# First stage and output products of a two-layer encoder trunk: rows turned by TensorE, written-out engine orders in the chunk loop, and a later place for the dilated heads' products

## The chip, the cores and the metric

The kernel runs on one core of a Trainium2 chip. A core has five engines that run their own instruction lists side by side: PE (TensorE, matmuls), ACT (ScalarE, functions and copies), DVE (VectorE, elementwise and reductions), POOL (GpSimd, elementwise from SBUF alone) and SP, which here only issues DMAs. They wait for each other by semaphores. The metric is the device time of one execution in microseconds (us), smaller is better.

## The reference, cut to what matters

Two layers of a bidirectional encoder on 512 tokens of width 1024. The conditioning vector c gives six vectors per layer (shift, scale and gate, twice).

```
c_act = silu(c)
for l in range(2):
    sh1, sc1, gt1, sh2, sc2, gt2 = split(c_act @ w_mod[l] + b_mod[l])
    h = rms_norm(x, g_norm_mix[l]) * (1 + sc1) + sh1
    q_d, k_d, v_d, cq, ckv, k_rope = split(h @ w_in[l])
    o_dil = dilated_attention(q_d, k_d, v_d, positions, slopes)   # 8 heads, biased by distance
    o_mla = latent_attention(cq, ckv, k_rope, positions, ...)     # 8 heads, rotary part with sin/cos
    x = x + gt1 * (concat[o_dil, o_mla] @ w_out[l])
    h = rms_norm(x, g_norm_mlp[l]) * (1 + sc2) + sh2
    x = x + gt2 * (square(relu(h @ w_mlp_in[l])) @ w_mlp_out[l])
```

## The kernel before, in words

x is kept transposed in SBUF as eight tiles of 128 features by 512 tokens. Every large product is made in float32 precision from three matmuls: each operand is split into a rounded high part and the rest, and `mm3` (lines 240 to 245) adds high times high (L241), one low part (L244) and the other low part (L245). `load_split` loads a weight tile by DMA into `raw` (or `zz`), ACT rounds it into `wh` (L233) and POOL makes the low part `wl` (L234).

**First stage (lines 86 to 154).** c is loaded column by column (`cs`), silu is made with Exp on ACT, and two matmuls with ones spread it over all partitions (`cb`). ACT squares the eight x tiles (L124, L127), DVE adds them up (L128) and a matmul with ones (L753) makes the sum of squares of each token. The positions are loaded as a column (`posc`), POOL makes and reduces the rotary angles (L135 to L147), ACT takes Abs and two Sin. Sin needs another function table than Exp and Ln: the table is loaded at L150 and put back at L152.

**Chunk loop of layer 0 (lines 750 to 780).** `inv_rms` (L250 to L256) turns the sum of squares into y = 1/rms: DVE scales the sum, ACT takes Ln (L252) and Exp (L253), DVE refines it in three steps. Then for each of eight chunks k of 128 features: DVE forms x times y (L759, L768), two modulation products with `cb`, one for shift and one for scale (L170, 128x1024 each), ACT makes the two columns from them (L194, L195), the rounded h (L772) and h in full (L773), and the low part of h is made by DVE for even chunks (L763) and by POOL for odd ones (L775). PE multiplies each chunk with the columns of W_in of the first pair of dilated heads (banks `mm`) and of the latent part (banks `sc` and `tr`), 24 matmuls in all, eight from each line of `mm3`. W_in comes in four double chunks, split by ACT and POOL (L233, L234). In this loop the order on DVE is the one in which the code is written (`tc.manual_schedule`); on all other engines, and everywhere else, the framework's list scheduler decides the order when the kernel is built. `W["tail"]` (L541 on) follows: turning the latent rows, the tables of the rotary part (`rope_tables`, L504 to L516, ten small POOL instructions called `rot`) and the rotated key (L559 to L562). `distances()` (L309 to L330) makes the distances between tokens.

**Pairs of heads.** Eight pairs of heads follow in each layer (`st` 0 to 7): four dilated pairs, four latent ones. A head has four blocks of 128 queries: scores on PE, maximum on DVE (L353), exponentials on ACT (L354), turning by PE (L365), split by ACT and DVE (L370, L371), values by PE (L377), and the head's end on DVE (L381). Beside pair st the next pair is prepared (`flow`), in layer 0 the other modulation products are made (`next_mod`), and the output product of the dilated heads, `out_dil(j)` for eight blocks j of 128 features, is put between: twelve matmuls of 128x512 each, and the addition to x on DVE (L670). `out_load(0, jj)` loads and splits its weights, two j each. `weave` and the numbers of TUNE say where in the program these stand: the number is how many blocks of the pair's two heads come first. The scheduler may move an instruction ahead of its place.

Of the kernel before, what the change touches and what calls it, by code (L numbers as in the profile page):

```python
# [42 lines left out]
def trunk(ctx: ExitStack, tc: tile.TileContext, a):  # L43
# [42 lines left out]
    cs = col(8, "cs")  # L86
    SY.dma_start(cs, a["c"].rearrange("(k p) -> p k", p=128))
    ident = const.tile([128, 128], F32, name="ident")
# [1 line left out]
    cols = [col(N_COL, f"cols{l}") for l in range(L)]  # L90
# [1 line left out]
    posc = const.tile([128, 4], I32, name="posc")
    SY.dma_start(posc, a["pos"].rearrange("(t p) -> p t", p=128))
    inv = col(16, "inv")
# [57 lines left out]
    pre = A.preload_act_table_set("natural_log_exp_and_others")  # L152
# [96 lines left out]
    def inv_rms(p, v, y, t):  # L249

        V.tensor_scalar(v, p, 1.0 / D, EPS, op0=OP.mult, op1=OP.add)
        A.activation(t, v, AF.Ln)  # L252
        A.activation(p, t, AF.Exp, scale=-0.5)  # L253
        V.tensor_tensor(t, v, p, op=OP.mult)
# [54 lines left out]
    def distances():  # L309

        posr = s2([128, S], I32)
        SY.dma_start(posr, bass.AP(tensor=a["pos"].tensor, offset=a["pos"].offset, ap=[[0, 128], [1, S]]))
        part = []
        for src, n, tile_ in ((posr, S, lambda dt: t4("pt", [128, 2, S], dt)),
                              (posc, 4, lambda dt: const.tile([128, 2, 4], dt, name=nm("pc")))):
            it, ft = tile_(I32), tile_(F32)
            V.tensor_scalar(it[:, 0], src, 16, None, op0=OP.arith_shift_right)
            V.tensor_scalar(it[:, 1], src, 65535, None, op0=OP.bitwise_and)
            V.tensor_copy(ft, it)
            part.append(ft)  # L320
        row, clm = part
# [66 lines left out]
    for l in range(L):  # L388
# [345 lines left out]
        if l == 0:  # L734
# [15 lines left out]
            with tc.manual_schedule(engines={mybir.EngineType.DVE}):  # L750
                for k in range(-1, 8):
                    if k < 0:
                        T.matmul(p, ones, sq0, start=True, stop=True)  # L753
# [10 lines left out]
                    if k < 7:  # L764
                        mod_block(0, k + 1, "ot", out=mraw[:, k + 1:k + 2])
                        if k < 0:
                            inv_rms(p, v, y, t)
# [6 lines left out]
                        if k % 2 == 0:  # L774
                            G.tensor_tensor(lo, u_of(k + 1), f(hi), op=OP.subtract)  # L775
# [213 lines left out]
```

## Time and profile before

| what | us |
|---|---|
| median of 3 runs | 1345.55 (1345.54 to 1348.59) |
| the profiled execution | 1343.71 |
| its span, first to last instruction | 1341.6 |
| start of the chunk loop's first matmul | 25.73 |
| start of the chunk loop's last matmul | 70.14 |
| end of head pair 1 / 4 / 8 in layer 0 (L381) | 134.2 / 227.9 / 331.2 |
| end of head pair 1 / 4 / 8 in layer 1 | 792.5 / 870.8 / 966.2 |

The profiled execution's time is 2.1 us longer than its span (what lies before the first and behind the last instruction) and 1.8 us under the median. The granted TensorE clock over the whole span is 0.984. A row of the timeline gives start, duration, engine, line, instruction and, in brackets, how long the engine had been idle and what ended that. A row of the windows gives for a stretch the busy time of PE, weight loads, DVE, ACT and POOL, the granted clock, the DMA share and rate.

### The profile page before, as it was taken

The page shows a single profiled execution, that of the slowest core. Times are in us where ns is not written, and L with a number is a line of the kernel's source. Part 1 is how long each engine was busy: PE and PEld are TensorE (multiplying, and loading weights), DVE is VectorE, ACT ScalarE, POOL GpSimd, SP SyncE. Part 2 cuts the span into 40 slices and gives each one's busy share as a digit, 9 for nine tenths or more (in the row PEclk, how much of TensorE's full clock was granted, in tenths as well). Part 3 has the DMA queues.
Part 4 walks back from the last instruction along what each step waited for, and adds up shares of the span by engine and source line. Part 5 has one row for each costly group of instructions (what it writes and reads, how often), then busy time and mean ns, then how long its engine had stood idle before and what let it go on. Part 6 is the DMA issues. An engine that isn't in the chain of part 4 may idle for free.

```text
span 1341.6 us, 19641 instructions
## 1 busy us (share of the span) xinstructions
PE 1263.8 (94%) x7114; PEld 1108.2 (83%) x7114; DVE 762.4 (57%) x1644; ACT 679.8 (51%) x1421; POOL 652.0 (49%) x504
## 2 busy tenths in 40 slices
PE   4879988988999999999999999899899999999998
PEld 2878867877998888888899999798799888888888
DVE  6777797886763661834476678987672121121223
ACT  5567898777632322322237677887663232232321
POOL 5646876674534444444438333545452444444441
PEclk7989999999999999999999999999999999999999
DMA  9335543332254572844434244211121222232221
GB/s 340 113 100 174 184 156 110 105 122 69 79 176 166 192 250 95 278 166 161 166 121 131 77 135 123 86 48 63 40 72 64 95 95 96 96 106 96 94 95 64
DMA packets 57248, 167.62 MB, mean 125 GB/s; under 512 B 8640, under 2 KB 10816, under 8 KB 57152
## 3 DMA queue, kind: packets, MB, share of 16 engines
q1 hardware_dynamic: 57152, 166.38, 37.2%
q8 instruction: 56, 0.92, 0.3%
q14 instruction: 40, 0.33, 0.1%
HBM read 155.87 MB, written 10.49 MB: 124 GB/s over the span
## 4 chain that ended last, share of the span: by engine, by line
PE 75%; DVE 6%; ACT 5%; DMA 3%; POOL 3%; issue 2%; DVEq 0%; ACTq 0%; POOLq 0%
PE mm L241 22%; PE mm L244 22%; PE mm L245 22%; PE tr L377 3%; PE tr L365 2%; DMA raw<-in_wout_dram 1%; DVE pt L371 1%; POOL wl L234 1%; DVE P L350 1%; ACT P L354 1%; PE sc L241 1%; ACT wh L233 1%; POOL raw L167 1%; PE sc L244 1%; PE sc L492 1%
## 5 line engine op out<-in xcount | busy, mean ns | idle before, releaser
L234 POOL TENSOR_TENSOR wl<-raw,wh 128x1024 fp32r<-128x1024 f32 (+3 forms) x174 | 395.2, 2273 | 434.4 <-ACT wh L233 431.1
L233 ACT ACTIVATE wh<-raw 128x1024 fp32r<-128x1024 f32 (+3 forms) x174 | 174.7, 1004 | 264.7 <-PE mm L245 212.0
L670 DVE SCALAR_TENSOR_TENSOR x<-mm,mod,x 128x512 f32<-128x512 f32 (+1 forms) x152 | 92.4, 621 | 255.1 <-PE mm L245 254.5
L241 PE MATMUL mm<-h,wh 128*128 128x512 f32 (+1 forms) x544 | 198.3, 364 | 0.0
L244 PE MATMUL mm<-h,wl 128*128 128x512 f32 (+1 forms) x544 | 198.1, 364 | 0.0
L245 PE MATMUL mm<-h,wh 128*128 128x512 f32 (+1 forms) x544 | 197.9, 364 | 0.0
L241 PE MATMUL mm<-ot,wh 128*128 128x512 f32 (+1 forms) x416 | 147.1, 354 | 0.8 <-DVE x L670 0.4
L865 ACT ACTIVATE P<-mm 128x512 f32<-128x512 f32 (+1 forms) x80 | 41.0, 513 | 210.3 <-PE mm L245 206.8
L245 PE MATMUL mm<-ot,wh 128*128 128x512 f32 (+1 forms) x416 | 143.7, 349 | 1.5 <-POOL ot L663 1.5
L244 PE MATMUL mm<-ot,wl 128*128 128x512 f32 (+1 forms) x416 | 144.9, 349 | 0.0
L866 DVE SCALAR_TENSOR_TENSOR mm<-mm,P 128x512 f32<-128x512 f32 (+1 forms) x80 | 46.9, 589 | 135.7 <-ACT P L865 135.7
L241 PEld LDWEIGHTS mm<-h,wh 128*128 128x128 f32 x544 | 102.7, 189 | 16.3
L244 PEld LDWEIGHTS mm<-h,wl 128*128 128x128 f32 x544 | 102.7, 189 | 16.1
L245 PEld LDWEIGHTS mm<-h,wh 128*128 128x128 f32 x544 | 102.6, 189 | 16.2
L241 PE MATMUL mm<-qk,wh 128*128 128x512 f32 (+1 forms) x288 | 105.3, 366 | 1.0 <-DVE x L670 1.0
L244 PE MATMUL mm<-qk,wl 128*128 128x512 f32 (+1 forms) x288 | 105.3, 365 | 0.0
L245 PE MATMUL mm<-qk,wh 128*128 128x512 f32 (+1 forms) x288 | 105.2, 365 | 0.0
L170 DVE SCALAR_TENSOR_TENSOR pt<-pt,cb 128x1024 f32<-128x1024 f32 x56 | 100.7, 1828 | 0.0
L371 DVE TENSOR_TENSOR pt<-tr,pt 128x512 fp32r<-128x512 f32 x128 | 86.6, 684 | 18.1 <-ACT pt L370 17.5
L362 POOL TENSOR_SCALAR P<-P,hs 128x512 f32<-128x512 f32 x64 | 48.1, 751 | 99.9 <-DVE hs L355 81.0
L241 PE MATMUL mm<-wh,h 128*128 128x384 f32 x240 | 81.3, 353 | 11.7 <-ACT h L772 9.8
L365 PE MATMUL tr<-ident,P 128*128 128x128 f32 x512 | 77.5, 275 | 15.7 <-DVE o L381 6.1
(290 smaller groups left out, 2968.9 us busy)
## 6 DMA issues: line engine op xcount, KB each, us to landing
raw<-in_w_dram SPq DMA_DIRECT2D x64, 512.0 KB, 3.4
pt<-in_wmod_dram SPq DMA_DIRECT2D x56, 512.0 KB, 4.8
raw<-in_w2a_dram SPq DMA_DIRECT2D x48, 512.0 KB, 3.5
raw<-in_wmod_dram SPq DMA_DIRECT2D x24, 512.0 KB, 3.6
raw<-in_win_dram SPq DMA_DIRECT2D x30, 384.0 KB, 3.0
bias<-b SPq DMA_DIRECT2D x32, 256.0 KB, 2.1
raw<-in_wout_dram SPq DMA_DIRECT2D x16, 512.0 KB, 3.7
raw<-in_w2b_dram SPq DMA_DIRECT2D x16, 512.0 KB, 3.4
```

The lines of the kernel that those rows point to most:

```text
L170: r = V.scalar_tensor_tensor(w, w, 1.0, cb, op0=OP.mult, op1=OP.mult, accum_out=out)
L233: ra = A.activation(hi, raw, AF.Copy)
L234: rg = G.tensor_tensor(lo, raw, f(hi), op=OP.subtract)
L241: r = T.matmul(out, sh, mh, start=first, stop=False)
L244: T.matmul(out, sl, mh, start=False, stop=False)
L245: T.matmul(out, sh, ml, start=False, stop=last)
L362: G.tensor_scalar(P, P, r_, 0.0, op0=OP.mult, op1=OP.add)
L365: T.transpose(tr[:, kc], P[:, kc * 128:(kc + 1) * 128], ident)
L371: V.tensor_tensor(lo, tr, f(hi), op=OP.subtract)
L670: V.scalar_tensor_tensor(xT[j][:, hf], p, gt[:, j:j + 1], xT[j][:, hf], op0=OP.mult, op1=OP.add)
L865: A.activation(r, p, AF.Relu)
L866: V.scalar_tensor_tensor(p, p, 0.0, r, op0=OP.max, op1=OP.mult)
```

## The change

Six edits. (1) c is loaded as 8 rows of 128 and the positions as 4 rows of 128, and PE turns them (one product with the identity for c, three for the positions with their two 16-bit halves); the column loads go away, and the halves that `distances()` needed come from the same product. (2) cos is made as the sine of pi/2 minus |angle|, with two small DVE instructions instead of Abs on ACT and a step on POOL; sine and cosine are one ACT instruction, which now stands behind chunk 1 of the chunk loop (`if k == 0`), with its table; the Exp table is put back behind the loop. (3) Ln in `inv_rms` reads the sum of squares itself, with scale and bias in the instruction, and no longer waits for the scaling on DVE. (4) In the chunk loop POOL and ACT, too, keep the order of the code, and the first double chunk of weights is split behind `inv_rms`. (5) The rotary tables and the rotated key become a step of their own (`rope`), in layer 0 at the second pair of heads. (6) `out_load(0, jj)` and `out_dil(j)` stand later: one product at the sixth pair, two at the seventh, five at the eighth, where there were two at each of the fifth to eighth; the loads for the latent half move from 0.5 to 5 to 2 to 6.

```diff
+    rows = s2([8, 4, 128], tag="b")
+    crow, prow, pi = rows[:, 0], rows[:4, 1].bitcast(I32), rows[:4, 2:].bitcast(I32)
-    SY.dma_start(cs, a["c"].rearrange("(k p) -> p k", p=128))
+    SY.dma_start(crow, a["c"].rearrange("(k p) -> k p", k=8))
     SY.dma_start(ident, a["ident"])
+    SY.dma_start(prow, a["pos"].rearrange("(t p) -> t p", t=4))
...
+    turn = ps("mm")
+    T.transpose(turn[:, :8], crow, ident[:8, :8])
-    A.activation(e, cs, AF.Exp, scale=-1.0)
+    A.activation(e, turn[:, :8], AF.Exp, scale=-1.0)
...
+    V.tensor_copy(parts[:, 2], prow)
+    V.tensor_scalar(pi[:, 0], prow, 16, None, op0=OP.arith_shift_right)
+    V.tensor_scalar(pi[:, 1], prow, 65535, None, op0=OP.bitwise_and)
+    V.tensor_copy(parts[:, :2], pi)
+    for i in range(3):
+        T.transpose(turn[:, 4 * i:4 * i + 4], parts[:, i], ident[:4, :4])
+    V.tensor_copy(clm, turn[:, :12].rearrange("p (i t) -> p i t", i=3))
...
-    A.activation(kf, ang, AF.Abs)
-    G.tensor_scalar(kf, kf, -1.0, math.pi / 2, op0=OP.mult, op1=OP.add)
-    A.activation(sin, ang, AF.Sin)
-    A.activation(cos, kf, AF.Sin)
-    pre = A.preload_act_table_set("natural_log_exp_and_others")
+    V.scalar_tensor_tensor(cos, sin, -1.0, sin, op0=OP.mult, op1=OP.min)
+    V.tensor_scalar(cos, cos, math.pi / 2, None, op0=OP.add)
...
     def inv_rms(p, v, y, t):
+        A.activation(t, p, AF.Ln, bias=epsc, scale=1.0 / D)
         V.tensor_scalar(v, p, 1.0 / D, EPS, op0=OP.mult, op1=OP.add)
-        A.activation(t, v, AF.Ln)
...
-            with tc.manual_schedule(engines={mybir.EngineType.DVE}):
+            with tc.manual_schedule(engines={mybir.EngineType.DVE, mybir.EngineType.Pool, mybir.EngineType.Activation}):
-                    elif k % 2 == 0:
+                    elif k % 2 == 0 and k:
                         PR[0]["load"][k // 2](raw=("raw", "zz")[k // 2 % 2])
...
                             inv_rms(p, v, y, t)
+                            PR[0]["load"][0](raw="raw")
+                            W["load"][0](raw="raw")
...
+                    if k == 0:
+                        A.activation(sines, sines, AF.Sin)
...
+            exp_tables()
...
-            if st >= 3 and st < 7:
-                ev += [(tn("LO"), lambda jj=st - 3: out_load(0, jj))]
-            if st >= 4:
-                ev += [(tn("OD0"), lambda j=2 * (st - 4): out_dil(j)), (tn("OD1"), lambda j=2 * (st - 4) + 1: out_dil(j))]
+            if 4 <= st < 7:
+                ev += [(tn("LO"), lambda jj=jj: out_load(0, jj)) for jj in {4: (0,), 5: (1,), 6: (2, 3)}[st]]
+            ev += [(at, lambda j=j: out_dil(j)) for at, j in {5: ((3.1, 0),), 6: ((3.1, 1), (5.1, 2)),
+                   7: ((0.6, 3), (1.6, 4), (2.6, 5), (3.6, 6), (4.6, 7))}.get(st, ())]
             if st == 7:
-                ev += spread([lambda jj=jj: out_load(1, jj) for jj in range(4)], tn("OL0"), tn("OL1"))
+                ev += spread([lambda jj=jj: out_load(1, jj) for jj in range(4)], 2, 6)
```

Where the change moves instructions, the built programs show it. On POOL in the chunk loop of layer 0, before (`wl` is a low part of weights, `h` the low part of an odd chunk, `rot` the rotary tables; numbers count up with the chunks):

```order
L234 TENSOR_TENSOR wl_232<-raw_230,wh_231 128x768
L234 TENSOR_TENSOR wl_238<-raw_236,wh_237 128x832
L234 TENSOR_TENSOR wl_316<-zz_314,wh_315 128x768
L234 TENSOR_TENSOR wl_322<-zz_320,wh_321 128x832
L775 TENSOR_TENSOR h_185<-pt_198,h_184 128x512
L234 TENSOR_TENSOR wl_400<-raw_398,wh_399 128x768
L775 TENSOR_TENSOR h_187<-pt_199,h_186 128x512
L775 TENSOR_TENSOR h_189<-pt_200,h_188 128x512
L511 TENSOR_TENSOR rot_732<-cos,gr_730 128x4x16
```

And on POOL at the same place now, from the second double chunk of weights on:

```order
L248 TENSOR_TENSOR wl_323<-zz_321,wh_322 128x768
L248 TENSOR_TENSOR wl_329<-zz_327,wh_328 128x832
L789 TENSOR_TENSOR h_193<-pt_205,h_192 128x512
L248 TENSOR_TENSOR wl_407<-raw_405,wh_406 128x768
L521 TENSOR_TENSOR rot_1319<-sines,gr_1317 128x4x16
L522 TENSOR_TENSOR rot_1319<-sines,gr_1317 128x4x16
L523 TENSOR_TENSOR rot_1320<-sines,gr_1317 128x4x16
L525 TENSOR_TENSOR rot_1320<-sines,gr_1317 128x4x16
L524 TENSOR_SCALAR rot_1320<-rot_1320 128x4x16
L248 TENSOR_TENSOR wl_413<-raw_411,wh_412 128x832
L789 TENSOR_TENSOR h_195<-pt_206,h_194 128x512
```

Before, the low part of chunk 5 (`h_189`) stood ahead of the rotary tables; now chunk 5's low part (`h_195`) and the latent weights of the third double chunk (`wl_413`) stand behind the first five of them. Behind these rows come the five other `rot`, the last two `wl` and the low part of chunk 7.

On ACT at the second double chunk of weights, before (`wh` is a rounded weight tile, `mod` and `am` the columns of shift and scale, `h` and `pt` a chunk rounded and in full):

```order
L772 ACTIVATE h_184<-pt_198,mod_167,am_169 128x512
L773 ACTIVATE pt_198<-pt_198,mod_167,am_169 128x512
L195 ACTIVATE am_169<-mraw_175,gb_173,cols_70 128x1
L233 ACTIVATE wh_315<-zz_314 128x768
L233 ACTIVATE wh_321<-zz_320 128x832
```

And now, from the rows of chunk 1 on:

```order
L787 ACTIVATE pt_204<-pt_204,mod_173,am_175 128x512
L791 ACT_TABLE_LOAD
L791 ACTIVATE sines<-sines 128x128
L208 ACTIVATE mod_173<-mraw_181,cols_70 128x1
L209 ACTIVATE am_175<-mraw_181,gb_179,cols_70 128x1
L786 ACTIVATE h_192<-pt_205,mod_173,am_175 128x512
L787 ACTIVATE pt_205<-pt_205,mod_173,am_175 128x512
L247 ACTIVATE wh_322<-zz_321 128x768
L247 ACTIVATE wh_328<-zz_327 128x832
```

Before, the second double chunk was rounded behind chunk 0; now it is rounded behind chunk 2, the first that needs it.

On DVE in layer 0, between the end of head 12 and the end of head 13 (the first head of pair 7), now (L391 ends a head, L682 adds an output product to x, L381 splits a turned block, L363 is a maximum):

```order
L391 TENSOR_TENSOR o_2807<-tr_3164,o_2807 64x512
L381 TENSOR_TENSOR pt_3188<-tr_3203,pt_3187 128x4x128
...
L682 SCALAR_TENSOR_TENSOR x_80<-mm_3606,mod_173,x_80 128x512
L682 SCALAR_TENSOR_TENSOR x_81<-mm_3639,mod_173,x_81 128x512
...
L682 SCALAR_TENSOR_TENSOR x_82<-mm_3678,mod_173,x_82 128x512
...
L682 SCALAR_TENSOR_TENSOR x_83<-mm_3717,mod_173,x_83 128x512
...
L682 SCALAR_TENSOR_TENSOR x_84<-mm_3750,mod_173,x_84 128x512
L391 TENSOR_TENSOR o_3186<-tr_3397,o_3186 64x512
```

Before, no output product stood between these two heads. Counted by heads in the order of DVE, the eight products of layer 0 stood 2, 2, 1, 3 in heads 9 to 12 and stand 0, 1, 0, 2, 5 in heads 9 to 13; those of layer 1 stood 2, 2, 1, 3 in its heads 9 to 12 and stand 0, 1, 1, 4, 2 in heads 9 to 13. So in both layers the scheduler brings them forward from the eighth pair to the sixth and seventh, and none stands in the eighth.

More of the change, by code (lines that the diff above doesn't have):

```diff
@@ L83, in col @@
         return const.tile([128, n], F32, name=nm(name))
[L86 to L88 removed]
+    rows = s2([8, 4, 128], tag="b")
+    crow, prow, pi = rows[:, 0], rows[:4, 1].bitcast(I32), rows[:4, 2:].bitcast(I32)
+    cs, ident, inv = col(8, "cs"), col(128, "ident"), col(16, "inv")
+    cols = [col(N_COL, f"cols{l}") for l in range(L)]
+    SY.dma_start(crow, a["c"].rearrange("(k p) -> k p", k=8))
     SY.dma_start(ident, a["ident"])
[L90 removed]
+    SY.dma_start(prow, a["pos"].rearrange("(t p) -> t p", t=4))
     SY.dma_start(cols[0], a["cols"][0])
[L92 to L94 removed]
     SY.dma_start(inv, bass.AP(tensor=a["inv"].tensor, offset=a["inv"].offset, ap=[[0, 128], [1, 16]]))
@@ L128, in trunk @@
             V.tensor_tensor(sq0, sq0, sq, op=OP.add)
-    pf = col(4, "pf")
-    V.tensor_copy(pf, posc)
-    ang, kf, w_ = s2([128, 4, 16]), s2([128, 4, 16]), s2([128, 4, 16], tag="b")
+    clm = const.tile([128, 3, 4], F32, name="clm")
+    parts = s2([4, 3, 128], tag="b")
+    V.tensor_copy(parts[:, 2], prow)
+    V.tensor_scalar(pi[:, 0], prow, 16, None, op0=OP.arith_shift_right)
+    V.tensor_scalar(pi[:, 1], prow, 65535, None, op0=OP.bitwise_and)
+    V.tensor_copy(parts[:, :2], pi)
+    turn = ps("mm")
+    for i in range(3):
+        T.transpose(turn[:, 4 * i:4 * i + 4], parts[:, i], ident[:4, :4])
+    V.tensor_copy(clm, turn[:, :12].rearrange("p (i t) -> p i t", i=3))
+    pf = clm[:, 2]
+    sines = const.tile([128, 2, 4, 16], F32, name="sines")
+    sin, cos = sines[:, 0], sines[:, 1]
+    ang, kf, w_ = sin, cos, s2([128, 4, 16])
     for t in range(4):
@@ L312, in distances @@
         SY.dma_start(posr, bass.AP(tensor=a["pos"].tensor, offset=a["pos"].offset, ap=[[0, 128], [1, S]]))
[L313 to L321, printed above, removed]
+        it = t4("pt", [128, 2, S], I32)
+        V.tensor_scalar(it[:, 0], posr, 16, None, op0=OP.arith_shift_right)
+        V.tensor_scalar(it[:, 1], posr, 65535, None, op0=OP.bitwise_and)
+        row = it.bitcast(F32)
+        V.tensor_copy(row, it)
         V.tensor_scalar(clm[:, 0], clm[:, 0], -65536.0, None, op0=OP.mult)
@@ L553, in tail, with rope @@
                     lat["CT"].append(ct)
+            def rope():
                 lat["Cq"], lat["Sq"] = rope_tables(a["gqr"][l], 0)
@@ L562, in tail @@
                 G.tensor_tensor(krot, krot, t1, op=OP.add)
-            w["tail"] = tail
+            w["tail"], w["rope"] = tail, rope
             return w
@@ L780, in trunk @@
                             W["step"](lbanks[tb][:, :W_C], k, tb)
+            exp_tables()
             gains()
@@ L803, in trunk @@
                 ev += spread(w["mm"][tb], 4 * n, 4 * n + 3.6) + [(4 * n + 3.8, w["chain"][tb])]
-            run(ev + [(tn("W0"), PR[0]["tail"][0]), (tn("W1"), PR[0]["tail"][1]), (tn("W2"), W["tail"])])
+            run(ev + [(tn("W0"), PR[0]["tail"][0]), (tn("W1"), PR[0]["tail"][1]), (tn("W2"), W["tail"]), (tn("W2"), W["rope"])])
         for st in range(8):
```

12 lines of the change are left out of this document (7 added, 5 removed).

## The prediction

> **What bounds the kernel now.** The page comes first, then the windows by stage, then the timeline of the first 90 us.
>
> ```profile
> PE 1263.8 (94%) x7114; PEld 1108.2 (83%) x7114; DVE 762.4 (57%) x1644; ACT 679.8 (51%) x1421; POOL 652.0 (49%) x504
> ...
> PE 75%; DVE 6%; ACT 5%; DMA 3%; POOL 3%; issue 2%; DVEq 0%; ACTq 0%; POOLq 0%
> ...
> 25.70:70.40 44.70, 39.92 (x192) 37.39 (x192) 33.74 (x46) 24.86 (x47) 28.77 (x23) 0.92 0.45 167
> ...
> 227.90:259.50 31.60, 29.80 (x192) 25.90 (x191) 27.03 (x65) 24.18 (x60) 17.46 (x25) 1.00 0.25 80
> 259.50:292.90 33.40, 31.43 (x194) 26.89 (x192) 27.24 (x66) 25.56 (x61) 24.23 (x31) 1.00 0.33 110
> 292.90:313.30 20.40, 15.74 (x91) 12.05 (x91) 16.11 (x30) 17.89 (x35) 13.51 (x9) 1.00 0.48 155
> 313.30:331.20 17.90, 16.07 (x121) 14.75 (x122) 11.29 (x23) 11.56 (x25) 8.08 (x6) 1.00 0.11 35
> ...
> 870.80:899.50 28.70, 28.70 (x190) 25.69 (x189) 23.07 (x58) 22.43 (x56) 15.07 (x22) 1.00 0.11 37
> 899.50:930.20 30.70, 30.41 (x191) 26.46 (x190) 24.07 (x59) 24.19 (x58) 16.41 (x21) 1.00 0.21 70
> 930.20:947.10 16.90, 15.06 (x91) 11.76 (x91) 12.26 (x26) 14.02 (x31) 5.19 (x6) 1.00 0.10 32
> 947.10:966.20 19.10, 16.13 (x121) 14.68 (x122) 11.38 (x24) 12.81 (x26) 7.45 (x5) 1.00 0.17 56
> ```
>
> PE is the bound over most of the span; the change keeps its large matmuls, so it can gain only where PE idles. The first row of windows is the chunk loop, the others are pairs 5 to 8 of heads in both layers (columns: length, busy PE, PEld, DVE, ACT, POOL, clock, DMA). Length less busy PE is 1.8, 2.0, 4.7 and 1.8 us in layer 0, and 0, 0.3, 1.8 and 3.0 us in layer 1. So moving the products can win at most 15.4 us, and only by filling the 11.3 us of pairs 7 and 8 without opening as much in pairs 5 and 6. The other place is the first 70 us.
>
> **The chunk loop is held by DVE and POOL together.**
>
> ```profile
> 19.99 3.71 POOL L234 TENSOR_TENSOR wl<-raw,wh 128x768 fp32r<-128x768 f32 x2 [3.34 <-ACT wh L233]
> 21.97 0.69 DVE L254 TENSOR_TENSOR b<-b,sc 128x512 f32<-128x512 f32 x1 [4.81 <-ACT sc L253]
> 24.75 0.68 DVE L759 TENSOR_TENSOR pt<-x,P 128x512 f32<-128x512 f32 x1
> 25.35 1.22 DVE L170 SCALAR_TENSOR_TENSOR qk<-qk,cb 128x1024 f32<-128x1024 f32 x1
> 26.49 0.08 DVE L170 DVE_READ_ACCUMULATOR qk<-qk,cb 128x1 f32 x1
> 27.81 4.68 POOL L234 TENSOR_TENSOR wl<-zz,wh 128x768 fp32r<-128x768 f32 x2 [4.11 <-ACT wh L233]
> 28.31 2.32 DVE L759 TENSOR_TENSOR pt<-x,P 128x512 f32<-128x512 f32 x1
> 30.56 3.01 DVE L170 SCALAR_TENSOR_TENSOR qk<-qk,cb 128x1024 f32<-128x1024 f32 x1
> 51.30 1.91 POOL L775 TENSOR_TENSOR h<-pt,h 128x512 fp32r<-128x512 f32 x1 [8.23 <-ACT pt L773]
> 53.91 1.30 POOL L512 TENSOR_TENSOR rot<-cos,gr 128x64 f32<-128x64 f32 x1
> 55.17 0.31 POOL L513 TENSOR_TENSOR rot<-sin,gr 128x64 f32<-128x64 f32 x1
> 64.15 1.84 POOL L234 TENSOR_TENSOR wl<-raw,wh 128x768 fp32r<-128x768 f32 x1
> 65.94 1.28 POOL L775 TENSOR_TENSOR h<-pt,h 128x512 fp32r<-128x512 f32 x1
> 67.27 0.46 PE L244 MATMUL mm<-wh,h 128*128 128x384 f32 x1 [0.43 <-POOL h L775]
> ```
>
> x times y takes 0.68 us alone and 2.32 us beside POOL's weight splits; a modulation product 1.22 and 3.01; a `rot` 0.31 and 1.30. Each lasts until the other's instruction is over, so the two engines take turns whenever DVE reads two operands from SBUF; L254, with one operand in PSUM, takes 0.69 us in the middle of POOL's pair. The Trainium skill says the same on its page "SBUF — State Buffer", section "Who interferes with whom": a DVE instruction with two SBUF inputs and a GpSimd one that reads SBUF exclude each other for the whole instruction. By that rule a new order cannot shorten this loop's shared work, which speaks against this edit; without it the loop would give rival B's time, and the trace agrees with the rule.
>
> Their turns add up. From starts one after another: modulation product 1.14 (25.35 to 26.49), x times y 0.6, DVE's low half 0.6, a pair of weight splits 3.7, POOL's low half 1.24 (65.94 to 67.18), a `rot` 0.28. The loop holds 14 x 1.14 + 8 x 0.6 + 4 x 0.6 + 4 x 3.7 + 4 x 1.24 + 10 x 0.28 = 45.7 us, and before also one split of the next pair's weights, 1.8: 47.5. Measured from the first split, 19.99, to the last low half, 67.2: 47.2. That resource is the loop's bound.
>
> **The change, part by part.** Edits 1 to 3, the start:
>
> ```profile
> 7.22 1.03 POOL L135 TENSOR_SCALAR s<-inv,pf 128x16 f32<-128x16 f32 x4 [6.78 <-PE sc L117]
> 10.96 3.16 DVE L128 TENSOR_TENSOR o<-o,P 128x512 f32<-128x512 f32 x4 [0.28 <-ACT P L127]
> 14.17 2.08 PE L753 MATMUL sc<-o,ones 128*128 128x512 f32 x2 [5.35 <-DVE o L128]
> 14.38 1.09 POOL L145 TENSOR_SCALAR s<-s 128x64 f32<-128x64 f32 x1
> 17.49 1.28 ACT L152 ACT_TABLE_LOAD   x1
> 20.00 0.61 ACT L252 ACTIVATE b<-b 128x512 f32<-128x512 f32 x1
> ```
>
> Ln waited at 20.00 behind table loads and a weight split, though its sum was there by about 16.5. Against that, the first of the two new cosine instructions stands on DVE ahead of the last of the seven additions, so the sum of squares waits for POOL's angles. These start about 0.6 later (c passes through PE, and DVE copies the turned columns behind its eight diagonals) and lose one step and the contention of the last, so they end near 14.4, and the sum near 15.2 instead of 14.1 (13.9 to 16.7 by the row of 14.38 with and without its contention). Then two modulation products and the scaling to 18.4, Ln and Exp to 18.6, three steps to 20.8; x times y gets its turn behind the first weight split at 21.3, and PE starts near 22.8 instead of 25.73. The column loads that go win nothing on this path: the additions at 10.96 waited for ACT and x.
>
> Edit 4: these 2.9 us are not kept, since the turns still add up: 19.5 + 45.7 = 65.2 for the last low half, against 67.2. And PE is fed worse. In the new order of POOL, five `rot` stand ahead of `wl_413` and of chunk 5's low part, and each gives DVE a turn. Ahead of `wl_413` the port has served five other splits and itself (11.1), two low halves (2.5), five `rot` (1.4), and on DVE 13 products, eight x times y, four low halves (22.0): 19.5 + 37.0 + 0.6 for moments in which both wait for ACT = 57.1 us. Between it and the split before lie 8.5 us of these turns, and on PE 16 matmuls, 3 us, so PE waits for some 5 us. Behind it PE still has 72 of 192 matmuls.
>
> ```profile
> 53.26 0.62 PE L244 MATMUL mm<-wh,h 128*128 128x384 f32 x1 [1.87 <-POOL h L775]
> 53.68 0.52 PE L245 MATMUL mm<-wl,h 128*128 128x384 f32 x1
> 54.00 0.52 PE L244 MATMUL mm<-wh,h 128*128 128x384 f32 x1
> 69.96 0.35 PE L244 MATMUL tr<-wh,h 128*128 128x416 f32 x1
> 70.14 0.35 PE L245 MATMUL tr<-wl,h 128*128 128x416 f32 x1
> ```
>
> 72 x 0.185 (69.96 to 70.14 and its like) is 13.3, and after a wait the first few run at 0.32 from start to start (53.68 to 54.00), about 1.6 more: 72.0, against 70.3. **Loop: +1.7.** Bounds: if POOL keeps its turn through the five `rot`, `wl_413` comes 5 us earlier and the last low half decides: 65.2 + 16 x 0.185 = 68.2, so -2.1; if the sum is 1.5 later and PE stays slow for longer, +4.
>
> Edits 2 and 5: the Sin table load and its way back cost 2.6 us of ACT where ACT waits for DVE; `rope` moves four small POOL instructions of 1.6 us from a gap. Both at nothing; if the gaps close, 1 us each. Edit 1 also takes the cast of positions ahead of a wait:
>
> ```profile
> 88.42 0.68 DVE L319 CAST pt<-pt 128x1024 f32<-128x1024 int32 x1
> 89.82 0.44 PE L241 MATMUL mm<-wh,h 128*128 128x384 f32 x1 [1.96 <-DVE ot L552]
> ```
>
> In the new order the cast stands ahead of the instruction that waits for PE, so the bank that PE waits for at 89.82 comes 0.7 earlier: **-0.7**. The order also puts about 2.5 us of preparing matmuls from heads 1 to 8 of layer 0 behind them; I take **-1.5** there (0 to -2.5; as a reshuffle it may also cost 3).
>
> Edit 6. A product is twelve matmuls:
>
> ```profile
> 926.66 0.39 PE L241 MATMUL mm<-h,wh 128*128 128x512 f32 x1
> 926.89 0.40 PE L244 MATMUL mm<-h,wl 128*128 128x512 f32 x1
> ```
>
> 0.23 apart, so 2.7 us each. Pair 5 of layer 0 goes from four to one, pair 6 from four to two, pair 7 from none to five, all in its first head. Pair 7's busy PE becomes 15.7 + 13.6 = 29.3, and half its idle stays: +9.4. Pair 5 would be 8.2 shorter if PE alone held it, but ACT is busy 24.2 of 31.6, and pair 7 before, with ACT at 88% of its length, shows how full ACT gets: 24.2 / 0.88 = 27.5, so about 28.3: -3.3. Pair 6 the same way, -3.6. **Layer 0: +2.5** (-2 to +7.4, the upper end if pairs 5 and 6 give back only 1 us each, the lower if pair 7's idle fills and pair 5 follows PE).
> Layer 1: pair 5 from four to one, 22.4 / 0.88 = 25.5: -3.2. Pair 6 from four to five, with some preparation moved ahead of it: +0.2. Pair 7 from none to two, 15.1 + 5.4 = 20.5: +3.6. Pair 8: -0.4. **Layer 1: +0.2** (-3 to +3).
>
> Sum: 1.7 - 0.7 - 1.5 + 2.5 + 0.2 = +2.2, so 1345.9 against the profiled 1343.71, and 1347.7 on the median of 1345.55.
>
> **The rivals.**
> B, faster: the shared port is not what holds the new loop. Then PE, from 22.8 with 192 x 0.185 and one slow start, would end near 60, and with the port partly in the way halfway to the lower bound, about 64: -6.1 instead of +1.7, 1339.9. For it: POOL idled 8.23 us up to 51.30, and 1.87 and 0.43 us of PE's waits were for POOL's order. Against it: the sum of turns that meets the trace within 0.3 us.
>
> C, slower: DVE and ACT hold pairs 5 and 6 at nearly their old length, so the products taken out leave idle PE and the five put into one head of pair 7 come on top. Layer 0 then costs 7.4 instead of 2.5, layer 1 about 1.3 more: +8.4, 1353.9. It decides once pair 5 of layer 0 stays over 30 us. For it: DVE busy 27.0 and ACT 24.2 of 31.6. Against it: in layer 1 PE has no idle at all there.
>
> D: the change does not do what it says. It half does not: the order shows the products in pairs 6 and 7, none in pair 8. That is in the sum already; its time is the forecast's.
>
> **How the numbers follow.** A measurement of this kernel tells about 0.3%, 4.0 us, from no change. Forecast with D: 45%, within 4 us of before; B 23%, faster by more; C 32%, slower by more: the loop's upper bound and layer 0's both lie there. Time 1347.7. The range leaves out half of B and the far end of C: 1339 to 1354. Faster 0.23, same 0.45, slower 0.32.
>
> **What would show it.** In the profile after: PE's first chunk matmul near 22.8; the chain of modulation products still stretched to 2 or 3 us beside POOL; a PE wait of some 5 us that ends on `wl` near 57; the loop's last matmul near 72. Pair 5 of layer 0 near 28 us, pair 7 near 30; layer 1's pairs 5 to 8 within 1 us of 95.4 in sum. I am wrong if the loop ends before 68 (the turns do not add up as I count), if the sum of squares comes after 17, or if pairs 5 to 8 of layer 0 come under 101 us (filled idle) or over 109.

## The result, and the profile after

| kernel | median, us | ratio to before, 95% interval |
|---|---|---|
| before | 1345.95 (4 runs, 1345.54 to 1348.59) | |
| changed | 1356.76 (4 runs, 1356.45 to 1361.85) | 1.0088 (1.0065 to 1.011) |

The changed kernel is slower by 10.8 us, against a forecast of 2.2 us and a range that ended at 1354. Its profiled execution took 1356.61 us with a span of 1354.8; that of before 1343.71 with 1341.6. The two profiles differ by 12.9 us.

The page of the changed kernel, busy time by engine and the chain that ended last:

```profile
PE 1270.9 (94%) x7118; PEld 1113.6 (82%) x7118; DVE 763.9 (56%) x1647; ACT 680.5 (50%) x1419; POOL 650.7 (48%) x503
...
PE 74%; DVE 8%; ACT 6%; DMA 3%; POOL 2%; issue 2%; DVEq 0%; ACTq 0%; POOLq 0%
```

PE is busy for 7.1 us more than before (1263.8) on the same matmuls, and DVE's share of the chain went from 6% to 8%. Where that lies is shown by the windows of the changed kernel: the chunk loop, head 7 of layer 0, pairs 5 to 8 of layer 0, pairs 5 to 8 of layer 1 (length, busy PE, PEld, DVE, ACT, POOL, clock, DMA):

```profile
22.60:70.10 47.50, 39.85 (x192) 36.80 (x192) 35.74 (x47) 27.60 (x50) 32.36 (x24) 0.93 0.50 185
192.20:217.00 24.80, 17.76 (x98) 14.25 (x97) 15.61 (x51) 20.61 (x52) 21.83 (x25) 0.85 0.40 127
230.80:263.50 32.70, 27.30 (x156) 22.94 (x155) 24.87 (x67) 24.60 (x63) 18.36 (x28) 0.84 0.28 77
263.50:293.60 30.10, 27.65 (x180) 24.38 (x181) 28.31 (x65) 24.23 (x60) 19.33 (x26) 1.00 0.31 101
293.60:324.10 30.50, 27.39 (x142) 22.42 (x140) 18.18 (x36) 20.18 (x38) 20.36 (x16) 0.94 0.45 141
324.10:342.30 18.20, 16.88 (x127) 15.53 (x128) 11.40 (x23) 12.14 (x25) 8.09 (x6) 1.00 0.15 50
881.90:907.20 25.30, 24.48 (x177) 22.53 (x178) 22.02 (x57) 21.51 (x58) 10.90 (x20) 1.00 0.06 22
907.20:939.50 32.30, 31.60 (x188) 27.32 (x187) 23.12 (x57) 23.84 (x54) 18.18 (x21) 1.00 0.21 66
939.50:960.70 21.20, 19.45 (x111) 15.30 (x109) 13.67 (x29) 15.15 (x32) 7.61 (x7) 1.00 0.15 50
960.70:979.50 18.80, 16.88 (x127) 15.41 (x128) 11.31 (x24) 12.92 (x26) 7.42 (x5) 1.00 0.15 46
```

Pairs 5 to 8 of layer 0 last 111.5 us instead of 103.3, those of layer 1 97.6 instead of 95.4. Head 7 of layer 0 lasts 24.8. Before, it was

```profile
195.70:213.30 17.60, 11.71 (x65) 8.82 (x66) 9.18 (x28) 14.26 (x30) 16.70 (x20) 0.81 0.48 158
```

that is 17.6 with a third fewer matmuls in it. Head 1 ends at 116.6 us instead of 117.0, and from layer 0's last head to layer 1's first it takes 444.2 us in both. So all of the loss lies in the heads: +3.2 in heads 2 to 8 of layer 0, +8.2 in heads 9 to 16, +2.2 in layer 1. Taken as one stretch, the end of head 1 to the end of head 16 in layer 0, the windows of before:

```profile
117.00:331.20 214.20, 191.15 (x1208) 167.18 (x1207) 169.01 (x406) 169.95 (x392) 142.55 (x143) 0.98 0.39 127
```

and of the changed kernel:

```profile
116.60:342.30 225.70, 198.07 (x1209) 173.75 (x1208) 169.99 (x406) 170.57 (x394) 140.73 (x147) 0.94 0.39 122
```

The work is the same (1208 and 1209 matmuls, DVE, ACT and POOL within 2 us). Of the 11.5 us more, 6.9 are longer busy time of the same matmuls, at a granted clock of 0.94 instead of 0.98, and 4.6 are more idle PE (27.6 for 23.0). Nearly all of the lost clock is in pairs 5 to 8, before and now:

```profile
227.90:331.20 103.30, 93.03 (x596) 79.59 (x595) 81.67 (x182) 79.18 (x178) 63.29 (x70) 1.00 0.30 96
230.80:342.30 111.50, 99.22 (x603) 85.26 (x603) 82.76 (x189) 81.15 (x183) 66.14 (x74) 0.94 0.31 97
```

There PE is busy for 6.2 us more and idle for 2.0 more; heads 2 to 8 add 0.7 busy and 2.6 idle. Head 7 shows how such an idle time comes about. Rows of ACT and PE there (start, duration, engine, line, instruction, idle time before):

```profile
203.75 1.06 ACT L247 ACTIVATE wh<-raw 128x1024 fp32r<-128x1024 f32 x1 [2.35 <-DMA raw<-in_wout_dram]
204.71 0.29 ACT L236 ACTIVATE st<-st,eps 128x12 f32<-128x12 f32 x1
204.91 0.71 ACT L368 ACTIVATE P<-P,hs 128x512 f32<-128x512 f32 x1
...
205.66 0.66 PE L375 MATMUL tr<-ident,P 128*128 128x128 f32 x4 [3.12 <-ACT P L368]
```

On ACT the split of the output weights waits 2.35 us for its DMA, the scaling of a block of probabilities stands two places behind it, and PE waits 3.12 us for that. That is one wait: most of head 7's extra time is work, 33 matmuls and 6.1 us of busy PE more, and 1.2 us is more idle. The clock falls in pair 5. Windows of 4 us for PE alone (length, busy, clock, DMA), the changed kernel in pair 5:

```profile
226.00:230.00 4.00, 3.61 (x30) 1.00 0.00 0
230.00:234.00 4.00, 2.54 (x12) 0.97 0.15 18
234.00:238.00 4.00, 2.50 (x7) 0.50 0.31 113
238.00:242.00 4.00, 3.13 (x11) 0.50 0.27 74
```

Before, at the same times:

```profile
230.00:234.00 4.00, 4.00 (x26) 1.00 0.37 113
234.00:238.00 4.00, 4.00 (x35) 1.00 0.05 20
238.00:242.00 4.00, 4.00 (x34) 1.00 0.56 185
```

There, with four output products in pair 5, 69 matmuls went through from 234 to 242 us at full clock; with one, and in the new order, 18 go through at half. Which of the two makes the difference is a question for the experiments.

The first stage did what the prediction said, only sooner. Rows of PE, DVE and POOL of the changed kernel:

```profile
14.30 2.08 PE L765 MATMUL sc<-o,ones 128*128 128x512 f32 x2 [5.48 <-DVE o L136]
22.63 1.65 PE L255 MATMUL mm<-wh,h 128*128 128x384 f32 x4 [6.25 <-ACT h L786]
37.05 2.99 DVE L184 SCALAR_TENSOR_TENSOR qk<-qk,cb 128x1024 f32<-128x1024 f32 x1
48.80 1.31 POOL L522 TENSOR_TENSOR rot<-sines,gr 128x64 f32<-128x64 f32 x1
53.25 1.94 POOL L248 TENSOR_TENSOR wl<-raw,wh 128x832 fp32r<-128x832 f32 x1
55.24 0.65 PE L259 MATMUL sc<-wl,h 128*128 128x416 f32 x2 [3.91 <-POOL wl L248]
62.89 1.29 POOL L789 TENSOR_TENSOR h<-pt,h 128x512 fp32r<-128x512 f32 x1
69.86 0.35 PE L259 MATMUL tr<-wl,h 128*128 128x416 f32 x1
89.25 0.45 PE L255 MATMUL mm<-wh,h 128*128 128x384 f32 x1 [1.67 <-DVE ot L562]
```

### The profile page after: what moved, and what is told of

Read it like the earlier page. It is cut to its first block, busy times and chain, and to the rows that moved or that the text cites. A ratio compares the mean times of both kernels' runs of the same rounds, so it can differ in the third digit from the quotient of the medians.

```text
span 1354.8 us, 19643 instructions
## 1 busy us (share of the span) xinstructions
PE 1270.9 (94%) x7118; PEld 1113.6 (82%) x7118; DVE 763.9 (56%) x1647; ACT 680.5 (50%) x1419; POOL 650.7 (48%) x503
## 4 chain that ended last, share of the span: by engine, by line
PE 74%; DVE 8%; ACT 6%; DMA 3%; POOL 2%; issue 2%; DVEq 0%; ACTq 0%; POOLq 0%
PE mm L255 21%; PE mm L258 21%; PE mm L259 21%; PE tr L387 3%; PE tr L375 2%; DVE pt L381 1%; DMA raw<-in_wout_dram 1%; DMA bias<-b 1%; DVE raw L184 1%; POOL wl L248 1%; ACT pt L380 1%; PE sc L255 1%; ACT P L364 1%; PE sc L502 1%; PE sc L258 1%
## 5 line engine op out<-in xcount | busy, mean ns | idle before, releaser
L682 DVE SCALAR_TENSOR_TENSOR x<-mm,mod,x 128x512 f32<-128x512 f32 (+1 forms) x152 | 92.5, 621 | 255.9 <-PE mm L259 255.5
L381 DVE TENSOR_TENSOR pt<-tr,pt 128x512 fp32r<-128x512 f32 x128 | 86.8, 683 | 24.4 <-ACT pt L380 23.4
```

What stands on the lines that cost most here:

```text
L381: V.tensor_tensor(lo, tr, f(hi), op=OP.subtract)
L682: V.scalar_tensor_tensor(xT[j][:, hf], p, gt[:, j:j + 1], xT[j][:, hf], op0=OP.mult, op1=OP.add)
```

## The experiments

Twelve kernels, each timed in four to eleven runs beside the kernel before on the same chip (its medians there 1344.4 to 1345.7). The lengths are from one profiled execution each, all of layer 0, from head end to head end; behind the heads of a layer (the MLP above all), where the instructions are the same, such profiles differ by up to 2 us through the granted clock alone, so a single pair says little below that. The profiled execution need not be a typical one either: it took 3.0 us less than its kernel's median in e2, and 3.9 more in e6 and 4.8 more in e10 (elsewhere it was within 2.3 us). The ratios rest on all runs, the lengths do not.

| kernel | ratio, 95% interval | head 7 | heads 2 to 8 | pairs 5 to 8 |
|---|---|---|---|---|
| before | 1 | 17.6 | 111.0 | 103.3 |
| changed | 1.0088 (1.0065 to 1.011) | 24.8 | 114.2 | 111.5 |
| e1 edit 6 alone | 1.0047 (1.0034 to 1.0059) | 12.7 | 111.3 | 104.3 |
| e2 edits 1 to 5 | 1.0058 (1.0044 to 1.0073) | 24.9 | 114.6 | 104.6 |
| e3 all but edit 5 | 1.0045 (1.0033 to 1.0057) | 13.0 | 109.3 | 106.4 |
| e4 hand order on DVE alone | 1.0095 (1.008 to 1.0109) | 25.9 | 115.4 | 111.0 |
| e5 edits 1 to 4 | 1.0003 (0.9993 to 1.0013) | 16.9 | 110.7 | 102.9 |
| e6 edit 5 alone | 1.0066 (1.005 to 1.0081) | 25.2 | 114.4 | 110.2 |
| e7 other scratch tile | 1.0079 (1.0065 to 1.0093) | 14.2 | 115.2 | 106.1 |
| e8 products spread | 1.005 (1.0035 to 1.0065) | 17.3 | 113.9 | 108.1 |
| e9 shorter projection | 1.0067 (1.0053 to 1.0081) | 14.7 | 112.9 | 109.5 |
| e10 longer projection | 1.0094 (1.0077 to 1.0111) | 17.5 | 113.4 | 115.5 |
| e11 more matmuls in pair 5 | 1.0103 (1.0085 to 1.0122) | 25.4 | 115.3 | 114.1 |
| e12 key rotation early, order late | 1.0097 (1.008 to 1.0113) | 24.5 | 113.6 | 114.6 |

**Which edits cost: e1 to e4.** Theory M put the loss on the products (edit 6), rival N on the edits of the first stage.

e1, the kernel before with edit 6:

```diff
-            if st >= 3 and st < 7:
-                ev += [(tn("LO"), lambda jj=st - 3: out_load(0, jj))]
...
+            if 4 <= st < 7:
+                ev += [(tn("LO"), lambda jj=jj: out_load(0, jj)) for jj in {4: (0,), 5: (1,), 6: (2, 3)}[st]]
```

> The kernel before with edit 6 alone (the products and their weight loads put later); the first stage and rope as before. Theory M (the products' new places lose the time: the +8.2 us of layer 0's pairs 5 to 8 and the +2.2 of layer 1's): 1345.9 + 10.4 = 1356, layer 0's pairs 5 to 8 near 111 us in sum, pair 5 over 30 us at a granted clock under 0.9, and head 7 of layer 0 near its 17.6 us. Rival N (the first-stage edits reshuffled the order behind them, and edit 6 only looked guilty): 1347 to 1349, pairs 5 to 8 of layer 0 within 3 us of the old 103.3.

e2, the changed kernel with the same lines the other way round:

> The changed kernel with edit 6 undone (the products and their loads where they were); edits 1 to 5 stay. Theory M: the first stage gives -0.3, heads 1 to 8 of layer 0 about +3 if the reshuffle comes from rope's new place, the pairs behind as before: 1346 to 1349. Rival N: 1354 to 1357, with head 7 of layer 0 near 24 us and pair 5 of layer 0 over 30 us at a low clock though its products are back.

e3, the changed kernel with edit 5 undone:

```diff
             W["tail"]()
+            W["rope"]()
...
-            if l == 0 and st == 1:
-                ev += [(2, W["rope"])]
```

> The changed kernel with edit 5 undone in layer 0: the key rotation stands again directly behind the latent tail, ahead of the first pair of heads. If rope in pair 2 made head 7 of layer 0 jump from 17.6 to 24.8 us: head 7 back under 20, 1350 to 1353. If edit 6's loads of w_out (moved from pairs 4 to 7 into pairs 5 to 7) or the products did it: head 7 stays over 23, 1355 to 1358. The order puts four products instead of five into the first head of pair 7; by theory M that saves at most one product's 2.7 us there.

e4, the changed kernel with a shorter list of engines:

```diff
-            with tc.manual_schedule(engines={mybir.EngineType.DVE, mybir.EngineType.Pool, mybir.EngineType.Activation}):
+            with tc.manual_schedule(engines={mybir.EngineType.DVE}):
```

> The changed kernel with the hand order of the chunk loop kept on DVE alone; POOL and ACT are ordered by the scheduler again. If the turns of DVE and POOL on their shared port bound the loop (as the prediction summed them), the loop's last matmul stays within 1.5 us of 69.9 and the time within 2 us of 1356.8. If the hand order of POOL and ACT costs or wins the loop's time (rival B's mechanism), the last matmul moves by 3 us or more, to under 67 or over 73, and the time with it.

Neither M nor N holds alone: edit 6 costs 0.47% by itself and the rest 0.58%. The rest is edit 5: without it (e3) head 7 falls to 13.0 us and half of the loss is gone. (Heads 6 and 7 together take 32.1 us before, 38.2 in the changed kernel and 31.0 in e3.) And edit 6 alone does not do what M said. Its pairs 5 to 8 of layer 0 are 104.3, not 111, with pair 5 at 28.5 and full clock. Its products stand 0, 1, 0, 2, 4, 1 in heads 9 to 14 (as in e3, e7 and e9), where the changed kernel has 0, 1, 0, 2, 5, 0. The windows of e1, pairs 5, 6 and 7:

```profile
227.70:256.20 28.50, 23.09 (x152) 19.76 (x152) 23.66 (x59) 21.36 (x55) 16.71 (x21) 1.00 0.27 86
256.20:282.90 26.70, 25.14 (x164) 21.89 (x164) 22.93 (x58) 23.57 (x59) 16.48 (x24) 1.00 0.35 103
282.90:313.90 31.00, 28.53 (x156) 23.69 (x156) 21.62 (x40) 21.27 (x41) 22.82 (x21) 1.00 0.44 151
```

and of e2, pair 5:

```profile
230.00:260.60 30.60, 28.92 (x186) 25.04 (x185) 25.97 (x64) 23.96 (x59) 17.89 (x25) 1.00 0.27 82
```

Not all that e1 costs lies in the heads. Of the 5.6 us by which its span is longer, the heads make some 2 (layer 1's pairs 5 to 8 take 97.6 us instead of 95.4); the other 3.5 lie behind the heads of the two layers, where the instructions are the same. One stretch of about 3.4 us at half clock stands in each place, the first of them

```profile
352.30:355.70 3.40, 3.40 (x19) 3.40 (x17) 3.01 (x8) 2.57 (x6) 3.15 (x6) 0.51 0.14 58
```

In e2, e3 and e6 2 to 4 us lie there too, in the changed kernel nothing. With one trace of each kernel it is open whether the order or the chance of the run puts such a stretch there (the profile of e5, below, has one as well, and its time is that of before). So the 0.47% is the price of edit 6 as timed, and the heads explain less than half of it.

e2 has head 7 at 24.9 and the first part of the loss, but with four products back in pair 5 that pair is 2.1 us shorter than in the changed kernel with one. e4 leaves the time where it was; its last loop matmul came at 68.13, just outside the 1.5 us, of which more below.

**Edit 5 by itself: e5 and e6.** e5 is e2 and e3 together; e6 is the kernel before with edit 5.

> The changed kernel with edits 5 and 6 undone: only the start, the chunk loop and the cast are changed, and the order behind them is that of before. Theory O (the whole loss is a new order behind the loop: 5.6 to 7.7 us through rope's new place, some 6 through edit 6, and what the start wins is kept): head 1 of layer 0 ends 0.4 to 1.6 us earlier and all that follows is as before, so 1344.4 less 0.4 to 1.6 = 1342.8 to 1344.0. Rival S (the start itself costs something behind the loop): 1347 or more.

> The kernel before with edit 5 alone: the key rotation goes into pair 2 of heads, nothing else. Theory O: heads 5 to 8 of layer 0 last 64 to 65 us instead of 58.7, with the last block of the fourth pair's projection in head 6 and head 7 near 25 us; 1350 to 1353. Rival P (rope costs only its own 1.6 us of POOL, and edits 1 to 4 together with it made the jump): under 1347.

Theory O holds in both, but not in its sizes. With edits 1 to 4 alone the order behind the loop is that of before, and so is the time, 1345.51 instead of the 1342.8 to 1344.0 expected; head 1 ended at 117.2 in that profile, so that what the start wins was not seen. Edit 5 alone costs 0.66% and head 7 is 25.2, but its 1355.02 is above O's 1350 to 1353, and heads 5 to 8 took 62.9 us, not 64 to 65. The output products move with it, though their places in the program are the old ones: two stand in head 13, which had none before (2, 1, 1, 2, 2 in heads 9 to 13; e2 has 2, 2, 0, 2, 2), and pair 7 takes 26.7 us instead of 20.4. Its pairs 5 to 8 are 110.2 us, those of e2 104.6; e6 was profiled in a long run and e2 in a short one, so that this difference says little. P has fallen.

**Why a step of 1.6 us on POOL costs that: e7, e9, e10 and e12.** With edit 5 the scheduler projects the last block of the fourth dilated pair one head later, and the first latent products move from head 6 into head 7. Matmuls by the head in which they run, those of the projection with `wh` and those of the latent part with `wh`:

| kernel | projection, heads 4, 5, 6 | latent, heads 5, 6, 7, 8 |
|---|---|---|
| before | 44, 16, 0 | 0, 24, 5, 19 |
| changed, e12 | 40, 8, 16 | 0, 2, 22, 24 |
| e2 | 40, 8, 16 | 0, 8, 16, 24 |
| e6 | 41, 13, 10 | 0, 6, 18, 24 |
| e3 | 43, 16, 0 | 0, 24, 0, 24 |
| e7 | 28, 36, 0 | 2, 22, 0, 24 |
| e9 | 40, 24, 0 | 0, 24, 0, 24 |
| e10 | 36, 28, 0 | 0, 24, 0, 24 |

(Some records of matmuls are missing.) So the experiments put these back in different ways.

e7:

```diff
-                t1 = s2([128, 4, 2, 16])
+                t1 = s2([128, 4, 2, 16], tag="b")
```

> The changed kernel whole, with one word different: the scratch tile of the key rotation comes from the ring of bias tiles (b) instead of that of squares (s); rope stays in pair 2. If the place of rope as such costs the time (POOL busy there, or its 1.6 us): head 7 stays near 25 us and the time at 1356. If the scratch tile does it, which takes one of two buffers that the projections' squares need, so that the scheduler puts the fourth pair's last block a head later: heads 5 to 8 fall under 60 us and the time to 1348 to 1351, as with rope put back.

e9 and e10, in layer 0 at `st` 2:

```diff
-                ev += flow(nx, tn("F0"), tn("F1")) + [(tn("T0"), nx["tail"][0]), (tn("T1"), nx["tail"][1])]
+                ev += flow(nx, tn("F0"), 5.4 if (l, st) == (0, 2) else tn("F1")) + [(tn("T0"), nx["tail"][0]), (tn("T1"), nx["tail"][1])]
```

> The changed kernel, rope in pair 2, with one number different: the fourth pair's projection in layer 0 is spread to step 5.4 of the third pair instead of 6.4. The scheduler then puts its last block back into head 5, the latent products of pair 5 back into head 6, and the products as 0, 1, 0, 2, 4, 1 over the heads 9 to 14, as with rope put back. Theory O (the order behind rope costs, not rope): heads 2 to 8 of layer 0 within 1.5 us of the kernel with rope put back (109.3), 1348 to 1352. If the late rotation itself costs: heads 2 to 8 stay over 113, 1354 to 1357.

> The same with that number 6.9: the last block of the fourth pair's projection is back in head 5 too, but the products stay as in the changed kernel, 0, 1, 0, 2, 5, 0. If the late block makes heads 2 to 8 long and the five products in one head make pairs 5 to 8 long, each for itself: heads 2 to 8 near 110, pairs 5 to 8 still 109 to 112, time 1352 to 1354. If the two go together (the order of pairs 5 to 8 costs only behind a late block): pairs 5 to 8 near 106, 1348 to 1351.

In e10 the first half of the fourth pair is turned before its second block is normalised, so heads 7 and 8 compute something else from the same amount of work.

The scratch tile alone is not it: e7 puts the latent products back into head 6, head 7 is 14.2 us and pairs 5 to 8 are 106.1, as in e3, but head 5 is 21.0 instead of 12.0 and heads 2 to 8 are no shorter. Its total says less: in layer 1, whose tile the word changes too, the way to the first head takes 451.5 us instead of 444.2 and heads 2 to 8 take 3.2 less, some 4 us that the changed kernel does not lose. The late block is not it alone either: in e9 the block and the latent products stand as in e3, and so do the output products by heads, and it is still 3.6 us longer than e3 in heads 2 to 8 and 3.1 in pairs 5 to 8. With 1353.99 and 112.9 it lies between its two expectations. e10 has the block back and keeps the products of the changed kernel; with 113.4 and 115.5, and 1356.45 in time, it missed both of its own. Pairs 5 to 8 with five products in one head are long without the late block too, though the 115.5 comes from a profile 4.8 us over the median.

e12, the changed kernel with the key rotation ahead of the heads again:

```diff
             bias0 = distances()
...
+            W["rope"]()
...
-            if l == 0 and st == 1:
-                ev += [(2, W["rope"])]
```

> The changed kernel with the key rotation issued ahead of the first pair of heads again, but behind the distance tables instead of ahead of them. On POOL its four instructions then run before the first head, as in the kernel before and with rope put back; the scheduler's order of PE behind it is still that of the changed kernel (the fourth pair's last block in head 6, the products 0, 1, 0, 2, 5, 0). If rope's late work on POOL costs the 6 us (129 to 132 us in head 2): head 2 back to 17.2, 1349 to 1352 as with rope put back. If the order behind it costs them: heads 2 to 8 of layer 0 stay at 113 or more, head 7 near 25, pairs 5 to 8 near 111, 1355 to 1358.

This settles what it could: on POOL the rotation runs at 85 us, before the first head, where e3 has it too, and the time is still that of the changed kernel. Head 2, in which the late rotation ran, takes 19.4 us as in the changed kernel (19.5), not 17.2; the time of 1358.16 and the pairs 5 to 8 lie a little over what was expected. Rows of POOL in e12:

```profile
84.75 0.84 POOL L571 TENSOR_TENSOR rot<-kr,rot 128x128 f32<-128x128 f32 x1 [11.72 <-DVE kr L546]
85.55 0.32 POOL L572 TENSOR_TENSOR s<-kr,rot 128x64 f32<-128x64 f32 x1
```

and its windows, head 7 and pair 5:

```profile
191.10:215.60 24.50, 17.15 (x97) 13.35 (x97) 15.53 (x50) 20.64 (x52) 21.65 (x25) 0.84 0.36 123
229.40:262.10 32.70, 27.51 (x156) 23.11 (x156) 24.91 (x68) 24.72 (x63) 18.36 (x28) 0.84 0.26 78
```

So the late work on POOL is not what costs. What is left is the order that the scheduler makes of everything behind it when this step stands at another place in the program, behind `distances()` as much as in pair 2.

**The products: e8 and e11.** e8 is e5 with these places in layer 0:

```diff
+            if l == 0:
+                ev += [(at, lambda jj=jj: out_load(0, jj)) for at, jj in {4: ((3, 0),), 5: ((3, 1), (7.2, 2)), 6: ((7.2, 3),)}.get(st, ())]
+                ev += [(at, lambda j=j: out_dil(j)) for at, j in {4: ((7, 0),), 5: ((2, 1), (4, 2), (6, 3)), 6: ((3.1, 4), (5.1, 5)), 7: ((2.1, 6), (5.1, 7))}.get(st, ())]
```

> Edits 1 to 4, rope in its old place, layer 1's products as before, layer 0's spread over the heads 9 to 14 as 1, 2, 1, 2, 2, 0 instead of 2, 2, 1, 3, 0, 0. If pair 7's idle PE (4.7 of 20.4 us before) can take two products without loss: pairs 5 to 8 of layer 0 near 101 and 1341 to 1342.5, faster than before. If a product there costs its 2.7 us of PE in full and pairs 5 and 6 win less than that: 1344 to 1347.

1351.71 was above both. Pair 7 takes its two products for 2.4 us, but pair 5 is 35.0 with three of them, and heads 2 to 8 are 2.9 longer though only a load of weights (that of pair 4) was taken out of them: here too the loads and products of later pairs change the order ahead of them.

e11 keeps PE at work where its clock fell:

```diff
+        def warm():
+            p = ps("mm")
+            for i in range(8):
+                T.matmul(p, OT[0][:, 0, :128], OT[0][:, 0], start=i == 0, stop=i == 7)
...
+            if l == 0:
+                ev += [(at, warm) for at in {4: (4.2, 5.2, 6.2)}.get(st, ())]
```

> The changed kernel with 24 matmuls 128x512 more in head 9 of layer 0, whose sum nobody reads: 24 x 0.23 = 5.5 us of PE at full clock, in the place of the products that went; all else as it was, the products too. If pair 5 is slow there because PE has too little to do and is granted half its clock (0.50 from 234 to 242): the clock stays near 1.00 and pair 5 stays at 31 to 33 us, with 5.5 us more work, or gets shorter. If PE's work holds it: 36 to 38 us and 1360 or more. Rival C (DVE and ACT hold it): 32 to 34 with the clock at 1.00 and PE's matmuls short, so that the clock was no cause.

The windows of e11 for pair 5:

```profile
232.20:265.60 33.40, 30.09 (x180) 26.17 (x179) 24.58 (x68) 25.45 (x65) 18.05 (x26) 0.95 0.27 81
```

and for PE alone in 4 us:

```profile
234.00:238.00 4.00, 3.85 (x17) 1.00 0.44 131
238.00:242.00 4.00, 4.00 (x21) 1.00 0.01 2
```

The clock at 234 to 242 us is back at 1.00, and pair 5 takes 24 matmuls more, 5.5 us by the estimate, in 0.7 us more time. That is the first theory's mechanism, but pair 5 got no shorter: 33.4 lies just outside that theory's 31 to 33 and inside rival C's 32 to 34. The half clock and the dummy work cost about the same, so the run doesn't tell whether pair 5 would be faster at full clock with nothing added. C is not out either: of the 5.4 us that PE idles in pair 5 of the changed kernel, most ends on ACT's exponentials (total us, times, longest):

```profile
PE sc L255 <- ACT P L364: 4.2, 4, 1.4
```

What e1 and e3 show is that pair 5 with one product can take 28.5 and 28.9, at a clock of 1.00 and of 0.94.

## Why the prediction was wrong, step by step

- **The start**: right at its end, partly by luck. The sum of squares came at 14.3, 0.9 sooner than expected (15.2), and the way from there to PE's first chunk matmul took 0.7 longer: 22.63 (22.8).
- **The loop, +1.7**: the mechanism right, the size off by 2.0. From the first split, 19.30, to the end of the last low half, 64.18, it takes 44.9 us where the turns added up to 45.7; DVE and POOL still stretch each other's instructions (2.99 and 1.31). PE waits for `wl` as said, 3.91 us up to 55.24 instead of 5 up to 57.1, and the last matmul starts at 69.86 instead of 72.0: -0.3. e4 bears the turns out: with POOL and ACT left to the scheduler the order is another and PE starts at 25.27, and the last low half still ends at 64.15. Rows of PE and POOL in e4:

```profile
25.27 1.65 PE L255 MATMUL mm<-wh,h 128*128 128x384 f32 x4 [9.40 <-ACT h L786]
62.86 1.29 POOL L789 TENSOR_TENSOR h<-pt,h 128x512 fp32r<-128x512 f32 x1
68.13 0.35 PE L259 MATMUL tr<-wl,h 128*128 128x416 f32 x1
```

The 2.6 us that the hand order wins at PE's start are lost by the end, and 1.7 more.

- **The cast, -0.7**: the bank that PE waits for comes at 89.25 instead of 89.82, 0.3 more than the loop gave and not 0.7. Head 1 ends 0.4 earlier.
- **Edit 5, "both at nothing"**: this is the step that failed. I priced the four instructions that move (1.6 us of POOL) and found their cover. What I priced was not the price of the edit: alone it costs 0.66%, 8.9 us (e6), the changed kernel stays as slow with the four instructions back at their old time on POOL (e12), and undoing the edit there (e3) gives back about half of the loss. In the sum the miss shows in two other terms: 5.7 us in pairs 5 to 8 of layer 0 and 4.7 in its heads 2 to 8; layer 1 adds 2.0 and the loop gives 2.0 back.
- **Heads 1 to 8 of layer 0, -1.5 (0 to -2.5, "as a reshuffle it may also cost 3")**: heads 2 to 8 took +3.2. I had read the new order and seen the preparation move, and took work that stands later for work that is hidden. It went into head 7, with 6.1 us more of busy PE there, and the heads before it gave back less.
- **Layer 0, pairs 5 to 8, +2.5 (-2 to +7.4)**: +8.2. For edit 6 alone the term was near: +1.0 in e1, with pair 5 at 28.5 (28.3 expected) but pair 6 at -6.7 (-3.6). Behind edit 5's order pair 5 stays at 32.7 at a clock of 0.84. Pair 6 (-3.3 for -3.6) and pair 7 (+10.1 for +9.4) came as said, pair 7 by luck: 29.3 us of busy PE and half of the 4.7 us idle are 31.6, which is +11.2 and not +9.4, so that the prediction's own working gives +4.3 for this term and +4.0 for the sum.
- **Layer 1, +0.2 (-3 to +3)**: +2.2. Pair 5 -3.4 (-3.2), pair 7 +4.3 (+3.6); pair 6 +1.6 instead of +0.2 is the term off.
- **The rivals**: B fell, the loop did not end before 68. C's condition came true, pair 5 over 30, and its 1353.9 was nearer than mine, but not for all of its reason: few products do not by themselves keep pair 5 long (28.5 and 28.9 in e1 and e3), and pair 6 did shorten. Whether ACT and DVE hold pair 5 in the order that edit 5 makes is open; e11 fits that, and so do the waits for ACT. D is as the order showed.

The two causes overlap: 0.47% for edit 6 and 0.66% for edit 5 by themselves, 0.88% together. What stays open is which moved instruction in heads 2 to 8 decides; e7 and e9 each put back what looked like it and lost most of it elsewhere. Open too is how much of a ratio comes from half-clock stretches outside the heads. No kernel here beat the one before; e5 equals it.

## What to carry to other kernels

Where a scheduler fills a stretch that is full on PE, an edit in the program text is priced by the order that comes out of it, head by head, and not by the instructions that it moves: of the thirteen kernels here only the one that left the order of the heads as it was (e5) cost nothing, and the others 0.45% to 1.03% (e11 with added work). Test each edit alone before pricing the sum, also the one that looks free. Taking work out of a stretch can cost idle time and then the clock, as in pair 5 of the changed kernel; e1 kept its clock there with as few products, so the order decides this too, and has to be read from a trace.
